# First layer of a two-block network: values stationary for two heads at a time, the gate z computed transposed, and a quarter of the adaLN rows multiplied on TensorE

## The chip, the cores and the metric

The kernel runs on one core of a Trainium2 chip. The metric is the device time of one execution in microseconds (us). The names of the engines are TensorE (PE, matrix products), VectorE (DVE), ScalarE (ACT), GpSimd (POOL) and SyncE (SP, which issues the DMAs here).

## What is computed

Two transformer blocks of two layers each, over 256 tokens of width 1024. The change lies in the mixer of the first layer, and in the rows of modulation that are computed beside it:

```python
def adaln_norm(x, c, g, w_ada, b_ada):
    mod = jax.nn.silu(c) @ w_ada + b_ada
    shift, scale, gate = jnp.split(mod, 3, axis=-1)
    h = rms_norm(x, g) * (1.0 + scale[:, None, :]) + shift[:, None, :]
    return h, gate[:, None, :]

def nsa_mixer(h, w_in, ..., w_out):
    u = h @ w_in
    q, k_c, v_c, k_s, v_s, k_w, v_w, z, g_logit = jnp.split(u, cuts, axis=-1)
...
    o = gates[..., 0:1] * o_cmp + gates[..., 1:2] * o_slc + gates[..., 2:3] * o_win
    o = o.reshape(B, T, ATTN_WIDTH)
    return (o * jax.nn.silu(z)) @ w_out

def first_block(x, c, norm_g, ada_w, ada_b, ...):
    for i in range(DEPTH):
        h, gate = adaln_norm(x, c, norm_g[i], ada_w[i], ada_b[i])
...
        x = x + gate * y
    return rms_norm(x, final_g)
```

The 16 heads of 64 share two groups of keys and values (8 heads each). `o_cmp` is an attention over 15 compressed keys, `o_slc` and `o_win` are here two causal attentions over the 256 tokens with keys and values of their own. All is float32.

## The kernel before

Weights come in units of 512 KB. Each unit is split into a high part (ScalarE, L210) and a low part (VectorE, L211), and the activations are held transposed, split likewise, in one tile `xhl` (channels on partitions). A dense product is three matmuls: high by high, low by high, high by low. `dense_cols` (L239, L240, L243) holds the activations of one token block (128 tokens) stationary and moves 512 columns of weights, so that tokens come out on partitions. `dense_T` (L297 to L299) holds 128 weight columns stationary and moves all 256 tokens, so that the result comes out transposed.

The stage of interest (lines 855 to 935, PSUM banks mm=[0], s=[1,2,3], pt=[4,5], o=[6,7]) computes the first layer's attention for key group g=1, then for g=0. For each group:

- The gate z of 512 columns comes from `dense_cols` (96 matmuls in all for both groups), then silu (ACT, then DVE L550) into `zs`, tokens on partitions.
- `cmp_part` (L885) starts the two accumulators `o` (one bank per token block) with the compressed attention.
- `nsa_pair` runs eight times, for four pairs of heads times two branches. Scores (L450, two heads in the two halves of the rows), mask and maximum (DVE L457), exponential (ACT L463), reciprocal and gate (DVE L894, L896), scaling (128 columns on DVE L904, 256 on ACT L902), then `av` for each head: three transposes (L470), a copy out of PSUM (ACT L473) and three matmuls 128x64 with the probabilities stationary (L476 to L478).
- After each pair, one (g=0) or two (g=1) steps of `ada_rows` make the rows gate0, scale and shift. A step takes a raw tile of 2 x 128 rows of the modulation weights by 512 columns (DMA, L619, three tiles `ar` in a ring) and adds them, scaled by silu(c), to `ac` (DVE L639, L641). Four steps are one half-row. Its end is one matmul by ones (L646), which sums over partitions, and one or two DVE operations (L649, L651, L652).

Then the z of group 1, already multiplied by `o`, and that of group 0 are transposed into `xhl` (`to_T`: L309 on TensorE into a pt bank, L312, L313). The output projection follows (`project_out`, accumulators y=[0,1,2,3], 96 matmuls by L239, L240, L243), the groups' rows 4 to 7 first. Its results go to `nsa_out` (L942 to L955): gate and residual (L378, L379), the norm (ACT L382, L947, POOL L334), scale and shift (L952, L953), transposes (L309), and then the second layer's first dense product.

The order in each engine's queue is set by a tile scheduler, which places instructions by a simulated timeline. `first(...)` gives priority, `behind(...)` puts one instruction after another. Buffers of a pool, PSUM banks among them, are handed out in the order in which the program asks for them. So the projection's products may be placed ahead of attention's last ones wherever their inputs and their banks are free.

## Time and profile before

| what | value |
|---|---|
| median of 3 runs | 999.81 us (993.23 to 1002.75) |
| the profiled execution | 996.02 us |
| its span in the profile | 994.2 us, 1.8 us less than the execution |
| mean granted TensorE clock | 0.978 of full speed |
| instructions | 14760 |
| TensorE busy | 939.6 us |
| VectorE busy | 697.2 us |
| ScalarE busy | 539.7 us |

The stage described above lies between about 96 and 228 us of the span. Times in the rows below are microseconds from the span's start; a line number is that of the listing above. Durations of matmuls overlap each other, since they are pipelined; what one costs is the distance from its start to the next one's. An fp32 matmul leaves two records, which the timeline counts as x2.

### The profile page before, as it was taken

Reading aid. Unit: us, or ns where it says so; the run is one execution under the profiler, and the core shown is the slowest. Engines: PE = TensorE matmul, PEld = TensorE weight load, DVE = VectorE, ACT = ScalarE, POOL = GpSimd, SP = SyncE. Lnnn points to the kernel's source line nnn. Section 1 sums busy time; section 2 is a strip of 40 time slices with the busy share of each in tenths; the row PEclk is TensorE's granted clock in tenths of the full one; section 3 lists DMA queues with packets and bytes.
Section 4 is the critical chain, followed back from the end, with each engine's and each line's share of the span. In section 5 each row is a group of like instructions: output and inputs, shape, how many; then the busy total and the mean of one; then the engine's idle time right before and its main releaser. Section 6 shows DMA issues by size and latency. Waiting matters only on the chain.

```text
span 994.2 us, 14760 instructions
## 1 busy us (share of the span) xinstructions
PE 939.6 (95%) x5316; PEld 787.7 (79%) x5316; DVE 697.2 (70%) x1446; ACT 539.7 (54%) x1062; POOL 40.7 (4%) x49
## 2 busy tenths in 40 slices
PE   5997999999999999999799999999999889999996
PEld 4876786687778877967788888887997688888885
DVE  5878799948786768585857565677466586665655
ACT  5574577834545636586346554435676345555540
POOL 1003000001220001000000000000000000000000
PEclk9998797999999999999999999999999999999999
DMA  9986687334865525732255554644635243564531
GB/s 288 309 290 230 202 278 248 120 107 131 267 198 180 157 59 194 250 114 86 94 203 212 169 184 158 245 177 152 220 130 158 85 169 124 188 239 170 182 136 43
DMA packets 106170, 177.66 MB, mean 179 GB/s; under 512 B 8817, under 2 KB 40689, under 8 KB 106097
## 3 DMA queue, kind: packets, MB, share of 16 engines
q1 hardware_dynamic: 106096, 176.72, 54.2%
q8 instruction: 42, 0.69, 0.3%
q14 instruction: 32, 0.25, 0.1%
HBM read 175.65 MB, written 1.05 MB: 178 GB/s over the span
## 4 chain that ended last, share of the span: by engine, by line
PE 78%; DVE 11%; ACT 4%; DMA 4%; issue 2%; SPq 1%; POOL 0%; DVEq 0%; ACTq 0%; POOLq 0%
PE ps L279 15%; PE ps L239 13%; PE ps L243 13%; PE ps L240 13%; PE ps L280 8%; DMA wr<-in_ada_w_dram 2%; PE ps L450 2%; DVE wl L211 2%; PE ps L320 1%; PE ps L820 1%; PE ps L309 1%; PE ps L506 1%; ACT e L463 1%; PE ps L297 1%; PE ps L298 1%
## 5 line engine op out<-in xcount | busy, mean ns | idle before, releaser
L211 DVE TENSOR_TENSOR wl<-wr,wh 128x1024 fp32r<-128x1024 f32 (+5 forms) x276 | 320.1, 1196 | 78.2 <-ACT wh L210 76.5
L210 ACT ACTIVATE wh<-wr 128x1024 fp32r<-128x1024 f32 (+5 forms) x276 | 270.6, 1021 | 72.9 <-PE ps L243 22.7
L279 PE MATMUL ps<-xhl,wh 128*128 128x512 f32 x640 | 226.5, 398 | 0.0
L239 PE MATMUL ps<-wh,xhl 128*128 128x512 f32 (+5 forms) x544 | 198.8, 379 | 5.1 <-ACT xhl L312 2.5
L240 PE MATMUL ps<-wl,xhl 128*128 128x512 f32 (+5 forms) x544 | 199.7, 370 | 0.0
L280 PE MATMUL ps<-xhl,wl 128*128 128x256 f32 x640 | 179.2, 281 | 0.0
L243 PE MATMUL ps<-wh,xhl 128*128 128x512 f32 (+5 forms) x544 | 173.5, 371 | 0.9 <-DVE xhl L313 0.6
L279 PEld LDWEIGHTS ps<-xhl,wh 128*128 128x128 f32 x640 | 120.0, 188 | 29.0
L239 PEld LDWEIGHTS ps<-wh,xhl 128*128 128x128 f32 x544 | 105.0, 194 | 23.7 <-ACT xhl L312 5.2
L280 PEld LDWEIGHTS ps<-xhl,wl 128*128 128x128 f32 x640 | 120.9, 189 | 1.1
L240 PEld LDWEIGHTS ps<-wl,xhl 128*128 128x128 f32 x544 | 105.2, 193 | 14.5 <-issue 0.5
L243 PEld LDWEIGHTS ps<-wh,xhl 128*128 128x128 f32 x544 | 100.2, 191 | 19.0 <-issue 2.7
L1105 ACT ACTIVATE hs<-ps 128x256 f32<-128x256 f32 x80 | 30.1, 379 | 100.6 <-PE ps L280 100.6
L1106 DVE TENSOR_TENSOR hs<-ps,hs 128x256 f32<-128x256 f32 x80 | 32.7, 421 | 69.4 <-ACT hs L1105 69.4
L243 PE MATMUL ps<-wh,hl 128*128 128x512 f32 x176 | 68.3, 390 | 0.0
L240 PE MATMUL ps<-wl,hh 128*128 128x512 f32 x176 | 68.3, 390 | 0.0
L239 PE MATMUL ps<-wh,hh 128*128 128x512 f32 x176 | 66.6, 390 | 0.0
L463 ACT ACTIVATE e<-e,sm 128x128 f32<-128x128 f32 x112 | 49.6, 445 | 10.4 <-DVE sm L457 10.1
L312 ACT ACTIVATE xhl<-ps 128x512 fp32r<-128x512 f32 x28 | 16.4, 597 | 66.8 <-PE ps L309 66.7
L457 DVE CUSTOM_DVE_ANT_0 e<-ps,mask 128x128 f32<-128x128 f32 (+1 forms) x144 | 44.4, 351 | 9.4 <-PE ps L436 4.6
L641 DVE SCALAR_TENSOR_TENSOR ac<-ar,cs,ac 128x512 f32<-128x512 f32 x56 | 42.7, 764 | 3.9 <-DMA ar<-in_ada_w_dram 3.6
L334 POOL TENSOR_TENSOR sm<-sm,nhalf 128x1 f32<-128x1 f32 x18 | 13.1, 730 | 723.1 <-DVE sm L333 723.1
(314 smaller groups left out, 1297.7 us busy)
## 6 DMA issues: line engine op xcount, KB each, us to landing
wr<-in_ffn_w_gate_dram SPq DMA_DIRECT2D x44, 512.0 KB, 4.5
wr<-in_ffn_w_up_dram SPq DMA_DIRECT2D x44, 512.0 KB, 4.8
wr<-in_ffn_w_down_dram SPq DMA_DIRECT2D x44, 512.0 KB, 4.9
ar<-in_ada_w_dram SPq DMA_DIRECT2D x32, 512.0 KB, 4.5
wr<-in_dil_w_in_dram SPq DMA_DIRECT2D x32, 512.0 KB, 4.7
wr<-in_cd_w_in_dram SPq DMA_DIRECT2D x22, 512.0 KB, 4.3
wr<-in_ada_w_dram SPq DMA_DIRECT2D x32, 256.0 KB, 5.0
wr<-in_nsa_w_in_dram SPq DMA_DIRECT2D x12, 512.0 KB, 5.1
```

The costliest lines, as they stand in the source:

```text
L210: act.activation(hi, raw[:, :nk * n], AF.Copy)
L211: dve.tensor_sub(lo, raw[:, :nk * n], hi.bitcast(F32))
L239: pe.matmul(p, lhsT=xt[0][:, k, :], rhs=w[0][:, kw, c], start=start and t == 0, stop=False)
L240: pe.matmul(p, lhsT=xt[0][:, k, :], rhs=w[1][:, kw, c], start=False, stop=False)
L243: pe.matmul(p, lhsT=xt[1][:, k, :], rhs=w[0][:, kw, c], start=False, stop=stop and t == n - 1)
L279: pe.matmul(p, lhsT=w[0], rhs=xhl[:, k].rearrange("p a t -> p (a t)"), start=k == 0, stop=False)
L280: pe.matmul(p[:, :256], lhsT=w[1], rhs=xh[:, k, :], start=False, stop=k == 7)
L457: state["dve"] = dve.tensor_tensor_reduce(out=e[:, c0:c1], in0=s[:, c0:c1], in1=added[:, 256 - (c1 - c0):], scale=-scale, scalar=3e38, op0 ...
L463: act.activation(e[:, c0:c1], e[:, c0:c1], AF.Exp, bias=n2[:, i:i + 1], scale=-1.0, accum_out=den[:, i:i + 1])
L641: dve.scalar_tensor_tensor(ac, raw[:, j, :], cs[:, k:k + 1], ac, op0=ALU.mult, op1=ALU.add)
L1105: act.activation(t[:, c], p[:, 256:], AF.Copy)
L1106: dve.tensor_add(t[:, c], p[:, :256], t[:, c])
```

## The change

1. z is computed by `dense_T` into `zT` (channels on partitions): 192 matmuls with 256 moving columns in place of 96 with 512. `to_T` on z is gone, `split_T` (L514 on ACT, L515 on DVE) splits `zT` into `xhl` without TensorE or PSUM.
2. `av` becomes `av_pair`, a helper that the later mixers use already. Values are stationary (64 columns), the transposed probabilities of a head move, and the two heads of a pair go to the two halves of the partitions of one bank: 4 matmuls (L506) in place of 6 for a pair, after the same 6 transposes. A bank of `o` now holds two pairs for all tokens, transposed.
3. `cmp_part` has 4 matmuls of 256 moving columns in a group in place of 2 of 512.
4. `ada_rows(..., own=6)`: the last two of the eight row blocks of a half-row are multiplied on TensorE (two fp32 matmuls with silu(c), broadcast over 128 columns, stationary, and the raw tile moving), into the bank where the matmul by ones then adds `ac`. The second layer's later call keeps own=8.

The new numbering moves the lines: L470 is now L495 (the helper's), L904 is L486, L930 is L935, L649 is L653; L646 is the new pair of matmuls and L647 the one by ones.

```diff
--- before.py
+++ after.py
@@ -605,7 +605,7 @@
 
     arow = {}
 
-    def ada_rows(rows, new, ahead):
+    def ada_rows(rows, new, ahead, own=8):
 
 
 
@@ -637,13 +637,17 @@
                     k = u * 2 + j
                     if k == 0:
                         dve.tensor_scalar(ac, raw[:, j, :], cs[:, k:k + 1], None, op0=ALU.mult)
-                    else:
+                    elif k < own:
                         dve.scalar_tensor_tensor(ac, raw[:, j, :], cs[:, k:k + 1], ac, op0=ALU.mult, op1=ALU.add)
+            if u == 3:
+
+                p = ps("pt")
+                for k in range(own, 8):
+                    pe.matmul(p, lhsT=cs[:, k:k + 1].to_broadcast([128, 128]), rhs=raw[:, k % 2, :], start=k == own, stop=False)
+                pe.matmul(p, lhsT=ones, rhs=ac, start=own == 8, stop=True)
             load()
             if u < 3:
                 return
-            p = ps("pt")
-            pe.matmul(p, lhsT=ones, rhs=ac, start=True, stop=True)
             dst, br = arow[name][:, half(h)], at["b"][:, half(h)]
             if at["g"] is None:
                 dve.tensor_add(dst, p, br)
@@ -672,7 +676,7 @@
     vbd = [np_.tile([128, 8, 64], F32, name=f"vbd{g}") for g in range(2)]
     qp = [[np_.tile([128, 4, 128], F32, name=f"qp{t}{g}") for g in range(2)] for t in range(2)]
     qr = [[np_.tile([128, 4, 128], F32, name=f"qr{t}{g}") for g in range(2)] for t in range(2)]
-    zs = [np_.tile([128, D], F32, name=f"zs{t}") for t in range(2)]
+    zT = np_.tile([128, 8, 256], F32, name="zT")
 
 
     cmA, a0 = opened("ada0")
@@ -854,7 +858,7 @@
 
     cmC, pC = opened("nsaC")
 
-    def cmp_probs(tok, g):
+    def cmp_probs(tok, g, t):
         p = ps("s")
         for pr in range(4):
             c = slice(pr * 30, (pr + 1) * 30)
@@ -877,12 +881,19 @@
         dve.tensor_mul(s, s, d8[:, :, None].to_broadcast([128, 8, NCMP]))
         pT = ps("pt")
         pe.transpose(pT[:120, :128], s.rearrange("p h n -> p (h n)"), ident)
-        t = pC.tile([128, 128], F32, tag="cT", bufs=4, name=nm("cT"))
-        act.activation(t[:120], pT[:120, :128], AF.Copy)
-        return t
+        act.activation(t[:120, tok, :], pT[:120, :128], AF.Copy)
+
+    def both_probs(g):
+        t = pC.tile([128, 2, 128], F32, tag="cT", bufs=2, name=nm("cT"))
+        for tok in range(2):
+            cmp_probs(tok, g, t)
+        return t.rearrange("p b t -> p (b t)")
 
     def cmp_part(t, g, o):
-        pe.matmul(o, lhsT=t[:120], rhs=vbd[g][:120].rearrange("p h d -> p (h d)"), start=True, stop=False)
+
+        for pr in range(4):
+            pe.matmul(o[pr // 2][:, (pr % 2) * 256:(pr % 2) * 256 + 256], lhsT=vbd[g][:120, 2 * pr:2 * pr + 2, :].rearrange("p h d -> p (h d)"),
+                      rhs=t[:120], start=pr % 2 == 0, stop=False)
 
     def nsa_pair(g, pr, br, o, last):
 
@@ -896,42 +907,34 @@
         dve.tensor_mul(rd.rearrange("p (j t) -> p j t", j=2), rd.rearrange("p (j t) -> p j t", j=2),
                        gates.rearrange("p t (h b) -> p h b t", b=3)[:, h:h + 2, 1 + br, :])
         for j, e in enumerate(es):
-            for i, (c0, c1) in enumerate(BLOCKS):
-                r = rd[:, 2 * j + i:2 * j + i + 1]
-                if i:
-                    act.activation(e[:, c0:c1], e[:, c0:c1], AF.Copy, scale=r)
-                else:
-                    dve.tensor_scalar(e[:, c0:c1], e[:, c0:c1], r, None, op0=ALU.mult)
-            av(e, lambda b: vv[:, b, g * 64:(g + 1) * 64], o, (pr * 2 + j) * 64, False, act, pC, stop=last and j == 1)
-
-    oxt = [None, None]
+            scaled(e, rd[:, 2 * j:2 * j + 2], (dve, act))
+        av_pair(es, lambda j, b: vv[:, b, g * 64:(g + 1) * 64], o[pr // 2], (pr % 2) * 256, (act, act), pC, False, last)
+
+    oxt = [xt_tiles(0), xt_tiles(1)]
     ada = ada_rows((("gate0", 0, 2 * D), ("scale", 1, D), ("shift", 1, 0)),
-                   lambda: pC.tile([128, D], F32, tag="araw", bufs=ARAW, name=nm("ar")), ARAW)
+                   lambda: pC.tile([128, D], F32, tag="araw", bufs=ARAW, name=nm("ar")), ARAW, 6)
     assign(mm=[0], s=[1, 2, 3], pt=[4, 5], o=[6, 7])
     with first(ATTN):
-        probs = [cmp_probs(tok, 1) for tok in range(2)]
+        probs = both_probs(1)
     for g in (1, 0):
         o = [ps("o"), ps("o")]
-        dense_cols(xt, 8, 512, lambda tok, p: silu2(p, zs[tok][:, half(g)], pC))
+        dense_T(512, lambda pair, p: silu2(p, zT[:, g * 4 + 2 * pair:g * 4 + 2 * pair + 2, :].rearrange("p k t -> p (k t)"), pC))
         with first(ATTN):
-            for tok in range(2):
-                cmp_part(probs[tok], g, o[tok])
+            cmp_part(probs, g, o)
             for i in range(8):
-                nsa_pair(g, i // 2, i % 2, o, i == 7)
+                nsa_pair(g, i // 2, i % 2, o, i in (3, 7))
                 for _ in range(1 + g):
                     ada(state["dve"])
                 if g and i == 3:
-                    probs = [cmp_probs(tok, 0) for tok in range(2)]
+                    probs = both_probs(0)
             if g == 0:
-                oxt = [xt_tiles(0), xt_tiles(1)]
-                for tok in range(2):
-                    to_T(zs[tok][:, half(1)], 4, oxt[tok], 4)
-            for tok in range(2):
-                dve.tensor_mul(zs[tok][:, half(g)], o[tok], zs[tok][:, half(g)])
+                for i in range(2):
+                    split_T(zT[:, 4 + 2 * i:6 + 2 * i, :].rearrange("p k t -> p (k t)"), 4 + 2 * i)
+            for i in range(2):
+                z = zT[:, g * 4 + 2 * i:g * 4 + 2 * i + 2, :].rearrange("p k t -> p (k t)")
+                dve.tensor_mul(z, o[i], z)
                 if g == 0:
-                    to_T(zs[tok][:, half(0)], 4, oxt[tok], 0)
-    for _ in range(24):
-        ada()
+                    split_T(z, 2 * i)
     closed(cmC)
 
     assign(y=[0, 1, 2, 3], pt=[6, 7])
```

How this moves instructions is seen in the engines' queues. In a row stand the line, the operation, output<-inputs with the numbers of the buffers, and the shape (output partitions x columns). `ps` is a PSUM bank, `eT` a head's transposed probabilities, `vS` and `vW` the values of the two branches, `wh` and `wl` the two parts of a weight unit, `cs` silu(c). TensorE in group 0, one pair's scores and a pair's products with the values, before:

```order
L450 MATMUL ps_2026<-kT,qr_114 128x128
L450 MATMUL ps_2025<-kT,qr_114 128x128
L450 MATMUL ps_2026<-kT,qr_116 128x256
L450 MATMUL ps_2025<-kT,qr_116 128x256
L470 MATMUL ps_1951<-ident,e_1936 128x128 x3
L470 MATMUL ps_1962<-ident,e_1942 128x128 x3
L476 MATMUL ps_1791<-vW,eT_1955 128x64
L477 MATMUL ps_1792<-vW,eT_1955 128x64
L478 MATMUL ps_1792<-vW,eT_1955 128x64
```

The same place after:

```order
L450 MATMUL ps_2101<-kT,qr_114 128x128
L450 MATMUL ps_2100<-kT,qr_114 128x128
L450 MATMUL ps_2101<-kT,qr_116 128x256
L450 MATMUL ps_2100<-kT,qr_116 128x256
L506 MATMUL ps_1822<-eT_1992,vS 64x256
L506 MATMUL ps_1822<-eT_1986,vS 64x256
L506 MATMUL ps_1822<-eT_1992,vS 64x128
L506 MATMUL ps_1822<-eT_1986,vS 64x128
L495 MATMUL ps_2038<-ident,e_2021 128x128 x3
```

Six products with the values in a pair (three are shown) have become four, of 64 partitions each, and one bank takes both heads. TensorE at the end of the stage, before:

```order
L646 MATMUL ps_2261<-ac_2118,ones 128x512
L476 MATMUL ps_1791<-vW,eT_2254 128x64
L477 MATMUL ps_1792<-vW,eT_2254 128x64
L478 MATMUL ps_1792<-vW,eT_2254 128x64
L309 MATMUL ps_2264<-ident,zs_118 128x128 x4
L309 MATMUL ps_2271<-ident,zs_119 128x128 x4
L239 MATMUL ps_2300<-wh_1254,xhl 128x512
L240 MATMUL ps_2300<-wl_1255,xhl 128x512
L239 MATMUL ps_2300<-wh_1254,xhl 128x512
```

The end of the stage after:

```order
L646 MATMUL ps_2324<-ar_2192,cs 128x512 x2
L506 MATMUL ps_1823<-eT_2318,vW 64x256
L506 MATMUL ps_1823<-eT_2312,vW 64x256
L506 MATMUL ps_1823<-eT_2318,vW 64x128
L506 MATMUL ps_1823<-eT_2312,vW 64x128
L647 MATMUL ps_2324<-ac_2189,ones 128x512
L239 MATMUL ps_2345<-wh_1921,xhl 128x512
```

Before, all 96 projection matmuls stood behind the last product with the values and behind the transposes of `zs`. After, the transposes are gone, and 72 of the 96 stand ahead of the last pair's products (12 of them ahead of the last pair's scores). TensorE's last rows ahead of the second layer, after:

```order
L243 MATMUL ps_2345<-wh_1921,xhl 128x512 x2
L243 MATMUL ps_2346<-wh_1945,xhl 128x512 x2
L243 MATMUL ps_2347<-wh_1921,xhl 128x512 x2
L243 MATMUL ps_2348<-wh_1945,xhl 128x512 x2
L309 MATMUL ps_2461<-ident,yt_2458 128x128 x4
L309 MATMUL ps_2471<-ident,yt_2468 128x128 x4
L239 MATMUL ps_2577<-wh_2369,xhl 128x512
```

Before, the four accumulators were finished one after the other; now the last eight matmuls finish all of them. VectorE in the last pair, before:

```order
L904 TENSOR_SCALAR e_2184<-e_2184,sm_2170 128x128
L457 ISA e_2230,sm_2229<-ps_2218,mask 128x128
L457 ISA sm_2229 128x1
L457 ISA e_2230,sm_2229<-ps_2218,mask 128x256
L457 ISA sm_2229 128x1
L641 SCALAR_TENSOR_TENSOR ac_2118<-ar_2121,cs,ac_2118 128x512 x2
L894 RECIPROCAL sm_2216<-sm_2215 128x4
L896 TENSOR_TENSOR sm_2216<-sm_2216,gates 128x4
L904 TENSOR_SCALAR e_2224<-e_2224,sm_2216 128x128
L904 TENSOR_SCALAR e_2230<-e_2230,sm_2216 128x128
```

VectorE in the last pair, after:

```order
L457 ISA e_2297,sm_2296<-ps_2285,mask 128x128
L457 ISA sm_2296 128x1
L457 ISA e_2297,sm_2296<-ps_2285,mask 128x256
L457 ISA sm_2296 128x1
L486 TENSOR_SCALAR e_2247<-e_2247,sm_2239 128x128
L486 TENSOR_SCALAR e_2253<-e_2253,sm_2239 128x128
L905 RECIPROCAL sm_2283<-sm_2282 128x4
L907 TENSOR_TENSOR sm_2283<-sm_2283,gates 128x4
L486 TENSOR_SCALAR e_2291<-e_2291,sm_2283 128x128
L486 TENSOR_SCALAR e_2297<-e_2297,sm_2283 128x128
L211 TENSOR_TENSOR wl_2370<-wr_2367,wh_2369 128x1024
```

The two operations L641 of a half-row's fourth step are not there any more; TensorE alone reads that step's raw tile (L646), so it is TensorE that frees it for a later load. VectorE behind the projection, before:

```order
L378 TENSOR_TENSOR yt_2388<-ps_2300,arow_1343 128x512
L379 TENSOR_TENSOR x_69<-x_69,yt_2388 128x512
L378 TENSOR_TENSOR yt_2404<-ps_2301,arow_1343 128x512
L379 TENSOR_TENSOR x_69<-x_69,yt_2404 128x512
```

The same place after:

```order
L378 TENSOR_TENSOR yt_2433<-ps_2345,arow_1389 128x512
L378 TENSOR_TENSOR yt_2449<-ps_2346,arow_1389 128x512
L379 TENSOR_TENSOR x_69<-x_69,yt_2433 128x512
L379 TENSOR_TENSOR x_69<-x_69,yt_2449 128x512
```

Gate and residual of the first token block's two halves now stand side by side, where one half was finished before the other began.

## Rows read from the trace of the kernel before

**Rows 1.** Stretch, its length; busy PE, PEld, DVE, ACT, POOL; granted clock; DMA share, GB/s

```profile
110.40:118.00 7.60, 7.25 (x29) 5.76 (x30) 5.90 (x25) 3.14 (x12) 0.00 (x0) 0.50 0.67 227
118.00:152.80 34.80, 34.80 (x220) 26.57 (x218) 33.77 (x107) 25.70 (x71) 0.00 (x0) 1.00 0.83 271
152.80:156.00 3.20, 1.63 (x12) 1.38 (x11) 3.20 (x7) 2.31 (x7) 0.00 (x0) 0.93 0.80 255
156.00:165.60 9.60, 9.60 (x39) 7.34 (x40) 7.69 (x32) 6.29 (x22) 0.00 (x0) 0.50 0.88 283
165.60:202.90 37.30, 34.01 (x255) 26.08 (x254) 31.34 (x126) 30.24 (x102) 0.00 (x0) 1.00 0.38 119
202.90:228.50 25.60, 25.20 (x122) 20.32 (x121) 15.32 (x23) 8.66 (x14) 0.55 (x1) 1.00 0.34 103
483.20:487.00 3.80, 3.78 (x17) 3.37 (x18) 3.77 (x8) 1.20 (x2) 0.92 (x1) 0.55 0.12 37
```

**Rows 2.** Waits of TensorE from 104 to 230 us, total, times, longest

```profile
PE ps L470 <- DVE zs L550: 1.3, 1, 1.3
```

**Rows 3.** Timeline of TensorE: start, length, instruction; xN records run together

```profile
135.84 0.33 PE L476 MATMUL ps<-vW,eT 128*128 128x64 f32 x2
...
136.45 1.08 PE L646 MATMUL ps<-ac,ones 128*128 128x512 f32 x2
137.36 0.30 PE L861 MATMUL ps<-kbd,qp 128*128 128x30 f32 x2
...
137.78 0.41 PE L476 MATMUL ps<-vW,eT 128*128 128x64 f32 x2
...
138.48 0.50 PE L470 MATMUL ps<-ident,e 128*128 128x128 f32 x3
...
397.68 0.28 PE L297 MATMUL ps<-xhl,wh 128*128 128x256 f32 x1
...
402.95 0.29 PE L299 MATMUL ps<-xhl,wl 128*128 128x256 f32 x1
...
443.34 0.87 PE L506 MATMUL ps<-eT,sv 128*64 128x256 f32 x8
444.14 0.50 PE L243 MATMUL ps<-wh,xhl 128*128 128x512 f32 x1
444.47 0.39 PE L239 MATMUL ps<-wh,xhl 128*128 128x512 f32 x1
```

**Rows 4.** Timeline from the last attention product to the next layer's first product

```profile
202.83 1.04 PE L309 MATMUL ps<-ident,zs 128*128 128x128 f32 x8
204.12 0.50 PE L239 MATMUL ps<-wh,xhl 128*128 128x512 f32 x1 [0.25 <-ACT xhl L312]
...
227.07 1.26 PE L309 MATMUL ps<-ident,yt 128*128 128x128 f32 x8
228.47 0.50 PE L239 MATMUL ps<-wh,xhl 128*128 128x512 f32 x1
...
221.72 0.69 DVE L378 TENSOR_TENSOR yt<-ps,arow 128x512 f32<-128x512 f32 x1 [1.30 <-PE ps L243]
```

**Rows 5.** The same place of the ab mixer, whose attention output is already transposed

```profile
471.23 0.87 PE L506 MATMUL ps<-eT,mv 128*64 128x256 f32 x8
472.80 0.50 PE L239 MATMUL ps<-wh,xhl 128*128 128x512 f32 x1 [0.70 <-ACT xhl L514]
...
478.19 0.39 PE L243 MATMUL ps<-wh,xhl 128*128 128x512 f32 x1
483.22 1.97 PE L309 MATMUL ps<-ident,x 128*128 128x128 f32 x8 [4.64 <-DVE x L367]
485.02 0.58 PE L239 MATMUL ps<-wh,xhl 128*128 128x256 f32 x1
```

**Rows 6.** Vector operations from 152.8 to 202.9 us, by line

```profile
L641 DVE SCALAR_TENSOR_TENSOR ac<-ar,cs,ac 128x512 f32<-128x512 f32 x24 | 17.9, 748 | 0.1
```

**Rows 7.** DMA of the raw adaLN rows from 96 to 204 us

```profile
DMA to landing us min/median/max: 3.6/4.4/6.2
```

## The prediction, made before the changed kernel ran

> **What bounds the kernel now.** TensorE is busy for 939.6 of the 994.2 us of the span, so the first question is where it is not at work, or not at full speed, in the stage that the change touches. I read the stage by stretches [rows 1], then the waits of TensorE [rows 2], then what one instruction costs, as the distance between starts [rows 3]. The reader should see three things. From 118.0 to 152.8 TensorE is busy all the time at granted clock 1.00 (2.4 GHz): there only its own work counts. From 165.6 to 202.9 it is busy for 34.01 of 37.3 us, VectorE for 31.34 and ScalarE for 30.24: a chain through all three engines, in which no single one is full. And in two stretches, 110.4 to 118.0 and 156.0 to 165.6, the granted clock is 0.50 (1.2 GHz). The second follows on an idle time of 1.3 us, in which a transpose L470 waited for the silu of z, VectorE's L550 [rows 2].
>
> I take one stretch for the whole balance, from 110.4 to 228.5, where the second layer's first product starts: 118.1 us. TensorE's idle time in it is length minus busy, row by row: 0.35 + 0 + 1.57 + 0 + 3.29 + 0.40 = 5.6 us. Of 7.6 + 9.6 = 17.2 us at half clock, half is lost: 8.6 us. The remaining 103.9 us are work at full clock. Everything outside the stretch (996.0 - 118.1 = 877.9 us of the profiled execution) I take as unchanged.
>
> **TensorE's work.** All durations are from [rows 3].
> - Products with the values: a head costs 0.61 us (135.84 to 136.45) or 0.70 (137.78 to 138.48), 0.66 as a middle, a pair 1.32. The new form stands in the later mixers: four matmuls L506 (eight records) take 0.80 (443.34 to 444.14). Sixteen pairs save 16 x 0.52 = 8.3 us (6.7 by the short head, 9.6 by the long).
> - Switching the shape of the array: behind such a group the next dense matmul starts 0.33 after the one before it (444.14 to 444.47), where 0.23 is usual (below). That is 0.1 for each pair, +1.6 us; the other end is nothing, since group 0 goes on to other small matmuls.
> - Transposes of z: eight took 1.04 us [rows 4], so the 16 that go save 2.1.
> - z itself: 192 matmuls of 256 columns at 0.120 (44 steps from 397.68 to 402.95) are 23.0; the 96 of 512 that go, at 0.234 (23 steps from 472.80 to 478.19 in [rows 5]), are 22.5. +0.5.
> - The compressed part has half the columns in twice the matmuls; I put it at nothing.
> - adaLN: twelve fp32 matmuls 128x512 more. The trace has none with a broadcast stationary. The matmul by ones has the same size and type, 0.91 (136.45 to 137.36). Bounds are 0.234, the cheap kind of the same size, and 1.82, as if loading the weights took as long again: 2.8 to 21.8 us. I take the nearest row, 0.91: +10.9.
>
> The sum is -8.3 + 1.6 - 2.1 + 0.5 + 10.9 = +2.6 us; TensorE, the fullest engine, gets more work, not less.
>
> Of the switch, the trace shows that the four matmuls and the way into them fit into 0.80 us. The Trainium skill, "TensorEngine Tiling (Array Packing)", Key Properties, says that a change of tiling mode drains TensorE. If each of two changes in a pair exposed a whole matmul latency (0.50 - 0.23 us, by the record at 444.14), that would be 16 x 2 x 0.27 = 8.6 us instead of 1.6, and the forecast 7.0 us later. The 0.33 us agrees with some drain, of a smaller size.
>
> **VectorE's work.** Twelve L641 of 0.748 us go [rows 6]: -9.0 us. Before 152.8 TensorE is full, so nothing comes of it there. Behind it, ScalarE's 30.24 us and TensorE's own work are next in line, so I leave the idle time of that chain at 3.29 us; the other end is that it vanishes. The raw tile of the fourth step is now freed by TensorE. A raw tile lands 3.6 to 6.2 us after its issue [rows 7]; three tiles are in the ring, so a step has about two others to cover that. In the queue the two matmuls stand in the middle of their pair, next to the preceding pair's products, and need no sum of VectorE's, so I price this at nothing; the cover is thin, and the second rival is what it costs without it.
>
> **The end of the stage.** Before, the path from the last product with the values ran 202.83 to 228.47, 25.6 us: transposes, 96 projection matmuls, transposes, next layer [rows 4]. After, 72 of the 96 stand ahead of that product, since their input needs no PSUM bank any more and the first half of it is ready when the second half's attention still runs. The ab mixer already has this form [rows 5]: last L506 at 471.23, a wait of 0.70 for the split, 24 matmuls to 478.4, an idle time of 4.64 for the norm, transposes. Here the norm differs. From the gate of token block 0's second half, L378 at 221.72, to the transposes at 227.07 it took 5.35 us [rows 4]. After, the gate and residual of both halves stand in front of it, 2 x 0.69 = 1.4 more, but the first starts some six matmuls (1.4 us) before the last one. I take 5.0, between 4.64 and 5.35. So the end is 0.70 + 5.6 + 5.0 + 1.4 (transposes to product, 227.07 to 228.47) = 12.7 us. Half of 25.6, but the 72 matmuls (16.8 us) are work still, only elsewhere; what is new in the balance is idle time of 0.70 + 5.0 = 5.7 in place of 0.40. The shorter end hides no VectorE work that was free before.
>
> **The sum.** Work 103.9 + 2.6 = 106.5. Idle 0.35 + 3.29 + 5.7 = 9.3, the 1.57 before the second slow spell being gone, since z's products of group 0 are spread over the pairs of group 1. Lost at half clock: the first spell's 3.8 stays; the second's 4.8 goes with the wait. Together 119.6, against 118.1: +1.5 us. On the profiled execution's own 996.0 this is 997.5 us. The median of the three runs is 999.8, 3.8 us above that execution; I do not add it. For this kernel a measurement can tell about 1% from no change, 10 us.
>
> **Rivals.**
> 1. Faster, the gaps fill. z's small matmuls also stand in the gaps ahead of 110.4, so the first slow spell may not come (-3.8); VectorE's 9.0 us empty the chain's gaps (-3.29); the work comes at its low end without switches (-2.9: long head and no switch). 997.5 - 10.0 = 987.5. For it: VectorE's L641 was the largest single group in that chain, 17.9 us [rows 6]. Against it: from 118 to 165.6 the DMA engines have a share of 0.80 to 0.88 [rows 1], so raw tiles come little sooner, and the three would all have to happen.
> 2. Slower, TensorE holds the raw tiles. If the two matmuls run more than a step behind VectorE, the ring's next load starts late; it lands 4.4 us later, two steps of two L641 each cover 3.0, and 1.4 us are left in which VectorE stands, with the reciprocal and the scaling of a pair queued behind L641, and TensorE behind these. That is the size of wait (1.3) after which the clock was at half for 9.6 us, 4.8 lost. So 6.2 us each time, and in group 1, with two steps a pair, there are three half-rows that another follows: two such events give 997.5 + 12.4 = 1009.9, one gives 1003.7. [...]
> 3. The clock falls at the new idle end. After the 4.64 us of ab the next product ran at granted clock 0.55 for 3.8 us (the last row of [rows 1]), 1.7 lost; 4.8 if it lasts like the spell at 156. 999.2 to 1002.3. The Trainium skill, "TensorE: Matmul & The Clock Gate", Part 1, has the throttled clock as the default that activity releases; that agrees with the row.
> 4. The change is a mere displacement: work comes out even, and idle time moves from the middle to the end. 996.0.
> 5. Each way into and out of the four matmuls exposes a whole latency, 0.27 us, 32 times: 8.6 us in place of 1.6, 1004.5. Against it: the 0.80 and 0.33 us of [rows 3].
>
> **Chances.** Forecast 0.33, rival 1 0.22, rival 2 0.15, rival 3 0.15, rival 4 0.10, rival 5 0.05. The forecast's own range is 988 (rival 1's terms) to 1004 (the wait of rows 2 comes back: 1.3 + 4.8). The broadcast matmul's bounds shift it by 8.1 down and 10.9 up. The range is 984 to 1010. Faster by over 1% needs rival 1 and a little more, or runs that lie as low as the profiled one: 0.22. Slower by over 1% is rival 2 with two events, or the dear matmul: 0.16. Within 1%: 0.62.
>
> **What would show it.** Right: L506 groups of 0.8 us, the broadcast matmuls at 0.9, VectorE 9 us less busy, an end of about 13 us from the last L506 to the next layer with some 5 us idle before L309, no half clock after 150. Wrong: TensorE waiting for L486 or L905 next to late raw tiles (rival 2); no half clock at all and a stage that reaches the second layer before 222 us (rival 1); broadcast matmuls far from 0.9.

## The result, and the profile after

The changed kernel took 1005.17 us (median of 22 runs, 1001.62 to 1007.72), the kernel before 998.03 in the same comparison (993.23 to 1003.90). The ratio is 1.0069, with an interval of 1.0053 to 1.0085: slower by 0.7%, where the forecast had 997.5 us. The profiled execution took 1007.39 us, its span is 1005.6.

The page of the changed kernel, busy us by engine and the granted clock in 40 slices of the span:

```profile
PE 943.7 (94%) x5364; PEld 786.2 (78%) x5364; DVE 690.3 (69%) x1434; ACT 539.2 (54%) x1062; POOL 40.6 (4%) x49
...
PEclk9998799998999999999899999999999979999999
```

VectorE's busy time fell from 697.2 to 690.3 us, TensorE's rose from 939.6 to 943.7. The same stretches as in [rows 1], in the columns stretch, length, busy PE, PEld, DVE, ACT, POOL, granted clock, DMA share, GB/s:

```profile
110.40:118.00 7.60, 7.17 (x38) 6.33 (x38) 5.75 (x25) 2.80 (x11) 0.00 (x0) 0.50 0.70 240
118.00:152.80 34.80, 33.13 (x241) 24.86 (x241) 30.49 (x105) 23.57 (x73) 0.00 (x0) 0.99 0.81 257
152.80:168.40 15.60, 13.86 (x101) 10.29 (x99) 12.58 (x33) 11.10 (x29) 0.00 (x0) 1.00 0.54 182
168.40:180.00 11.60, 11.04 (x57) 6.27 (x58) 9.13 (x38) 8.17 (x27) 0.00 (x0) 0.85 0.76 249
180.00:218.10 38.10, 37.03 (x221) 25.30 (x221) 24.20 (x88) 27.27 (x81) 0.00 (x0) 1.00 0.39 126
218.10:226.20 8.10, 7.67 (x35) 5.21 (x34) 3.33 (x6) 0.63 (x1) 0.00 (x0) 1.00 0.25 72
226.20:233.20 7.00, 1.87 (x9) 1.61 (x9) 4.82 (x10) 1.93 (x5) 0.55 (x1) 0.65 0.00 0
233.20:236.00 2.80, 2.80 (x10) 2.25 (x10) 2.80 (x5) 1.32 (x3) 0.00 (x0) 0.66 0.00 0
```

The stage now ends at 233.2 (228.5 before). From 110.4 on, TensorE's idle time by row is 0.43 + 1.67 + 1.74 + 0.56 + 1.07 + 0.43 + 5.13 = 11.0 us, 5.6 before. Low clock stands in the first row, as before, in part of the fourth and in the last two. The waits of TensorE from 90 to 240 us (total, times, longest):

```profile
PE ps L309 <- issue: 5.2, 1, 5.2
PE ps L495 <- DVE arow L655: 1.7, 1, 1.7
...
PE ps L297 <- DVE zT L550: 0.8, 1, 0.8
```

The wait of 1.3 us for L550 in [rows 2], which was to go, has shrunk to 0.8, but one of 1.7 us for the row of scale (L655) has come, and the clock was low just behind it, at 170 to 174. The trace shows why it came:

```profile
163.50 1.02 PE L647 MATMUL ps<-ac,ones 128*128 128x512 f32 x2
...
167.67 0.68 DVE L655 SCALAR_TENSOR_TENSOR arow<-ps,ab 128x512 f32<-128x512 f32 x1
168.41 0.55 PE L495 MATMUL ps<-ident,e 128*128 128x128 f32 x3 [1.75 <-DVE arow L655]
```

The sum was ready by 164.5, but VectorE went without a pause through two weight splits (L211), one `split_T` (L515) and one L641 before it read the sum (L655), and L655 is what the trace names as the releaser of the transposes L495. The prices of the new instructions, against [rows 3]:

```profile
130.37 0.87 PE L506 MATMUL ps<-eT,vS 128*64 128x256 f32 x8
131.17 0.55 PE L495 MATMUL ps<-ident,e 128*128 128x128 f32 x3
...
133.94 1.88 PE L646 MATMUL ps<-ar,cs 128*128 128x512 f32 x4
135.65 1.02 PE L647 MATMUL ps<-ac,ones 128*128 128x512 f32 x2
136.60 0.65 PE L506 MATMUL ps<-eT,vW 128*64 128x256 f32 x4
```

The products of a pair take 0.80 us (130.37 to 131.17), two broadcast matmuls 1.71 (133.94 to 135.65), so 0.86 each, and the matmul by ones 0.95. VectorE's share, against [rows 6]:

```profile
L641 DVE SCALAR_TENSOR_TENSOR ac<-ar,cs,ac 128x512 f32<-128x512 f32 x30 | 22.4, 747 | 2.7 <-DMA ar<-in_ada_w_dram 2.5
```

30 in the whole stretch, 42 before: twelve are gone. The end of the stage, against [rows 4] and [rows 5]:

```profile
218.11 0.87 PE L506 MATMUL ps<-eT,vW 128*64 128x256 f32 x8
...
220.43 0.50 PE L239 MATMUL ps<-wh,xhl 128*128 128x512 f32 x1 [0.40 <-ACT xhl L514]
...
224.20 1.98 PE L243 MATMUL ps<-wh,xhl 128*128 128x512 f32 x8
231.33 1.94 PE L309 MATMUL ps<-ident,yt 128*128 128x128 f32 x8 [5.16 <-issue]
233.16 0.79 PE L239 MATMUL ps<-wh,xhl 128*128 128x512 f32 x1
...
224.85 1.29 DVE L378 TENSOR_TENSOR yt<-ps,arow 128x512 f32<-128x512 f32 x2 [3.49 <-PE ps L243]
226.06 1.28 DVE L379 TENSOR_TENSOR x<-x,yt 128x512 f32<-128x512 f32 x2
228.14 0.16 DVE L950 TENSOR_TENSOR sm<-sm 128x1 f32<-128x1 f32 x1 [0.80 <-ACT junk L382]
...
229.21 1.41 DVE L955 SCALAR_TENSOR_TENSOR yt<-x,sm,arow 128x512 f32<-128x512 f32 x2 [0.73 <-POOL sm L334]
```

From the end of the last L506 (218.11 + 0.80) to the second layer (233.16) are 14.3 us, 12.7 were forecast; a matmul by ones stands in between. The idle time ahead of the transposes is 5.16 us, 5.0 were forecast. The rows of VectorE show what fills it: gate and residual of both halves, and the norm. The first products behind it run at half clock: L309 takes 1.94 us where [rows 4] has 1.26.

### The profile page after: what moved, and what is told of

It reads as the page before. It is cut to its first block, busy times and chain, and to the rows that moved or that the text cites. A ratio compares the mean times of both kernels' runs of the same rounds, so it can differ in the third digit from the quotient of the medians.

```text
span 1005.6 us, 14837 instructions
## 1 busy us (share of the span) xinstructions
PE 943.7 (94%) x5364; PEld 786.2 (78%) x5364; DVE 690.3 (69%) x1434; ACT 539.2 (54%) x1062; POOL 40.6 (4%) x49
## 4 chain that ended last, share of the span: by engine, by line
PE 78%; DVE 10%; DMA 4%; ACT 4%; issue 3%; SPq 1%; POOL 0%; DVEq 0%; ACTq 0%; POOLq 0%
PE ps L279 15%; PE ps L239 13%; PE ps L240 13%; PE ps L243 13%; PE ps L280 8%; PE ps L450 2%; PE ps L506 2%; DMA wr<-in_ada_w_dram 2%; PE ps L297 2%; PE ps L495 2%; DVE wl L211 2%; PE ps L299 2%; PE ps L298 2%; PE ps L320 1%; ACT wh L210 1%
## 5 line engine op out<-in xcount | busy, mean ns | idle before, releaser
L211 DVE TENSOR_TENSOR wl<-wr,wh 128x1024 fp32r<-128x1024 f32 (+5 forms) x276 | 320.2, 1196 | 80.1 <-ACT wh L210 78.0
L239 PE MATMUL ps<-wh,xhl 128*128 128x512 f32 (+5 forms) x512 | 186.4, 377 | 5.5 <-ACT xhl L312 2.5
L240 PE MATMUL ps<-wl,xhl 128*128 128x512 f32 (+5 forms) x512 | 189.7, 373 | 0.0
L280 PE MATMUL ps<-xhl,wl 128*128 128x256 f32 x640 | 179.2, 281 | 0.0
L243 PE MATMUL ps<-wh,xhl 128*128 128x512 f32 (+5 forms) x512 | 164.5, 373 | 0.8 <-DVE xhl L313 0.6
L239 PEld LDWEIGHTS ps<-wh,xhl 128*128 128x128 f32 x512 | 98.9, 195 | 23.2 <-ACT xhl L312 4.5
L240 PEld LDWEIGHTS ps<-wl,xhl 128*128 128x128 f32 x512 | 101.1, 197 | 13.3 <-issue 0.3
L243 PEld LDWEIGHTS ps<-wh,xhl 128*128 128x128 f32 x512 | 96.7, 196 | 16.5 <-DVE xhl L313 1.9
L312 ACT ACTIVATE xhl<-ps 128x512 fp32r<-128x512 f32 x24 | 14.2, 597 | 66.5 <-PE ps L309 55.0
L297 PE MATMUL ps<-xhl,wh 128*128 128x256 f32 x160 | 48.0, 300 | 0.8 <-DVE zT L550 0.8
L299 PE MATMUL ps<-xhl,wl 128*128 128x256 f32 x160 | 47.1, 294 | 0.9 <-DVE wl L211 0.9
```

What stands on the lines that cost most here:

```text
L211: dve.tensor_sub(lo, raw[:, :nk * n], hi.bitcast(F32))
L239: pe.matmul(p, lhsT=xt[0][:, k, :], rhs=w[0][:, kw, c], start=start and t == 0, stop=False)
L240: pe.matmul(p, lhsT=xt[0][:, k, :], rhs=w[1][:, kw, c], start=False, stop=False)
L243: pe.matmul(p, lhsT=xt[1][:, k, :], rhs=w[0][:, kw, c], start=False, stop=stop and t == n - 1)
L280: pe.matmul(p[:, :256], lhsT=w[1], rhs=xh[:, k, :], start=False, stop=k == 7)
L297: pe.matmul(o, lhsT=w[0], rhs=xh[:, k, :], start=k == 0, stop=False)
```

## Experiments

Two theories stood at first. A: the loss is TensorE's work for the adaLN rows. C: it is the new end. The expectations name rivals by letters too: B, VectorE is as full as TensorE there; D, the idle time only moves; E, what costs is that TensorE holds the raw tile and a bank. Besides the ratio of each run there is a narrower measure, the length of the stage in its one profiled execution: from the first product of the scores (L450, at 111.09 in the changed kernel, 110.75 before) to the second layer's first product. "Block 0 first" is the edit of run 4 below.

| run | median us | ratio, interval | stage us |
|---|---|---|---|
| before | 998 | | 117.7 |
| changed (own=6) | 1005.17 | 1.0069, 1.0053 to 1.0085 | 122.1 |
| 1: own=8 | 1000.84 | 1.0023, 1.0001 to 1.0046 | 117.1 |
| 2: before, own=6 alone | 1004.48 | 1.0065, 1.0038 to 1.0092 | 120.7 |
| 3: projection behind | 1002.52 | 1.0039, 1.0018 to 1.0059 | 119.3 |
| 3a: both 1 and 3 | 1000.28 | 1.0020, 0.9997 to 1.0042 | 116.4 |
| 4: block 0 first | 1000.72 | 1.0016, 0.9987 to 1.0045 | 118.0 |
| 4a: both 1 and 4 | 998.22 | 0.9989, 0.9953 to 1.0026 | 113.7 |
| 4a again | 997.78 | 0.9999, 0.9978 to 1.0021 | 114.4 |
| 5: own=7 | 1002.68 | 1.0026, 0.9996 to 1.0055 | 118.8 |
| 6: thin broadcast, behind | 1003.74 | 1.0032, 1.0001 to 1.0064 | 121.4 |
| 6a: thin broadcast, in place | 999.71 | 0.9990, 0.9968 to 1.0011 | 116.9 |
| 6b: own=8 and a thin read | 1004.12 | 1.0052, 1.0025 to 1.0079 | 120.9 |
| 7: bank of the scores | 1002.85 | 1.0041, 1.0021 to 1.0060 | 125.2 |
| 8: own=6 beside group 0, block 0 first | 999.35 | 1.0012, 0.9993 to 1.0031 | 116.5 |
| 8a: own=6 beside group 1, block 0 first | 999.51 | 1.0021, 1.0002 to 1.0040 | 115.9 |
| 8b: own=6 beside group 0, projection behind | 1002.68 | 1.0046, 1.0025 to 1.0067 | 119.6 |
| 9: GpSimd, block 0 first | 1006.73 | 1.0081, 1.0050 to 1.0112 | 123.3 |

Medians of different rows come from different hours; the ratios compare each with the kernel before on its own chip. A stage holds what its one execution lost to a low clock; the two of 4a differ by 0.7 us, and for run 7 stage and ratio point opposite ways.

**Runs 1 and 2: the adaLN rows alone.** Run 1 edits the changed kernel as below; run 2 gives the kernel before the new `ada_rows` with own=6, and nothing else:

```diff
-                   lambda: pC.tile([128, D], F32, tag="araw", ...), ARAW, 6)
+                   lambda: pC.tile([128, D], F32, tag="araw", ...), ARAW, 8)
```

> The changed kernel with own=8: the twelve broadcast matmuls go back to twelve L641 on VectorE, all else as changed. Theory A (the loss is TensorE's extra work for the adaLN rows, 12 x 0.9 = 10.9 us on the fullest engine): about 6 to 9 us less than the changed kernel, 996 to 999 us, VectorE 9 us more busy. Rival B (VectorE is as full as TensorE there, the 9.0 us come back on its side): 1004 to 1006, no difference from the changed kernel. Theory C (the loss is the new end, 5.2 us of idle time and the half clock behind it) says nothing of this part alone: the gap of about 5 us before the transposes stays in either case.

> The kernel before with own=6 alone: values, z and the end as before. Theory A: 4 to 9 us slower than before, 1002 to 1007 us. Rival B: VectorE's relief pays for TensorE's work, within 2 us of before, or faster. Theory C: no difference from before, since the end is the old one.

Taking the twelve matmuls out of the changed kernel gives back 4.6 thousandths (1.0069 to 1.0023) and 5.0 us of the stage; putting them into the kernel before costs 6.5. Theory A's size is right for run 2 and too large for run 1 (4.3 us between the medians, expected were 6 to 9), B falls. But own=8 is still no faster than before, though against the kernel before 8.9 us of TensorE's work are away (the balance below). Idle time took their place: 6.2 us more at the new end and some 4 in the chain ahead of it, as in the stretch from 155 to 170 of run 1 (columns as above):

```profile
155.00:170.00 15.00, 11.23 (x80) 7.38 (x78) 14.95 (x42) 12.22 (x34) 0.00 (x0) 1.00 0.90 295
```

VectorE is busy for 14.95 of 15 us, TensorE for 11.23.

**Runs 3 and 4: the end.** Run 3 puts every projection matmul behind the last product with the values. Run 4 leaves the early ones and puts only token block 1's last twelve behind those of block 0:

```diff
-                products(accs[tok][h], ..., start=not last, stop=last == 1, ...)
+                products(accs[tok][h], ..., start=not last, stop=last == 1, ...,
+                         late=state["mm0"] if late and last and tok else None)
+                if not tok:
+                    state["mm0"] = state["mm"]
```

where `late` stands ahead (`behind`) of the last two of four terms, and `state["mm"]` is the last matmul made.

> The changed kernel with all 96 projection matmuls behind the last product with the values, so that token block 0's accumulators are finished ahead of block 1's, as before. Theory C: the gap of 5.2 us before the transposes and the half clock behind it go, the last product with the values comes near 203 us instead of 218, and the second layer starts near 228 to 229 instead of 233: 997 to 1001 us. Rival D (the gap only moves: TensorE waits in the attention for what the early projection filled): last product with the values near 207 or later, 1003 to 1007 us.

> Both at once: own=8 and the projection behind the last product with the values. Theories A and C together: 988 to 994 us, faster than both kernels. B and D: no better than the better one of the two single edits, 997 or more.

> The changed kernel, with token block 1's last 12 projection matmuls behind block 0's last one, so that block 0's two accumulators are finished 12 matmuls (2.7 us) ahead of the end. The early projection stays. Theory C (the end's idle time is a loss of its own): the gap of 5.2 us before the transposes falls to some 2.5 to 3 and the half clock behind it shortens or goes; 1000.5 to 1003 us against 1005.2 for the changed kernel. Rival D (the gap only moves): 1004 to 1006.

> The same order of the last 24 matmuls with own=8. Theories A and C add up: 1000.8 (own=8 alone) less 2.5 to 4.5, 996 to 998.5 us, at or a little below the kernel before. Rival D: 1000 to 1001.5.

Run 3 lies between C and D, and with own=8 it adds almost nothing (1.0023 to 1.0020). The last product with the values came at 204.7, near C's 203, but what the early projection had filled was then idle, as D has it (8.8 us up to there, 5.5 in the changed kernel up to 218.1). Run 4 is C's clean form, and within its bounds: the idle time ahead of the transposes falls from 5.16 to 3.35 us,

```profile
225.72 1.67 PE L311 MATMUL ps<-ident,yt 128*128 128x128 f32 x8 [3.35 <-issue]
227.10 0.79 PE L240 MATMUL ps<-wh,xhl 128*128 128x512 f32 x1
```

and the stage by 4.1 us with own=6 and 3.4 with own=8 (table). By the ratios the order in which the last 24 matmuls finish the accumulators costs 5.3 thousandths with own=6 and 2.4 to 3.4 with own=8.

Runs 1 and 4 add up by the stage: with both, 113.7 us, 4.0 less than before; the end's order adds 3.4 (117.1), the adaLN rows 5.0 more (122.1). That is the whole change: -4.0 + 3.4 + 5.0 = +4.4 us. But 3.3 of the 4.0 us are low clock, of which before's profiled execution had more (8.7 us lost, 5.4 in run 4a's). By idle time and work alone (the balance below) the three steps are -0.9, +2.2 and +5.4: +6.7 us, of which the adaLN rows are the largest part.

**Run 5: half the rows.** `ARAW, 7)` in place of 6.

> The changed kernel with own=7: one row block of eight on TensorE, six broadcast matmuls in place of twelve. Theory A (each costs its time on TensorE, and VectorE's relief pays only part of it): half way between own=6 (1005.2) and own=8 (1000.8), 1002 to 1004 us. Rival B (two engines out of balance, an optimum between): below both, 999 or less.

It lies between own=8 and own=6, in stage and ratio, as A expected; no optimum between shows.

**Run 6: TensorE's time, or the hold?** The broadcast matmuls are cut to 64 of 512 columns, so that most of their products are left out: first behind the matmul by ones (run 6), then ahead of it as in the changed kernel (run 6a, the edit below, cut; a cheap bf16 matmul fills the bank first), then with own=8 (run 6b):

```diff
-                for k in range(own, 8):
-                    pe.matmul(p, lhsT=cs[:, k:k + 1].to_broadcast([128, 128]), rhs=raw[:, k % 2, :], ...)
-                pe.matmul(p, lhsT=ones, rhs=ac, start=own == 8, stop=True)
...
+                pe.matmul(p, lhsT=identb, rhs=identb[:, None, :].to_broadcast([128, 4, 128]), start=True, stop=False)
+                for k in range(6, 8):
+                    pe.matmul(p[:, 0:64], lhsT=cs[:, k:k + 1].to_broadcast([128, 128]), rhs=raw[:, k % 2, 0:64], ...)
+                pe.matmul(p, lhsT=ones, rhs=ac, start=False, stop=True)
...
```

> The changed kernel, in which the twelve broadcast matmuls read and add only the first 64 of 512 columns (behind the matmul by ones), so most of rows 6 and 7 of each eight is left out of gate0, scale and shift. TensorE's price is nearly gone, VectorE's relief of 9.0 us stays. Theory A: TensorE's 12 x 0.9 us were what cost, so 7 to 10 us below the changed kernel, 995 to 998. By its distance to own=8 (1000.8) VectorE's relief is measured: if it is worth nothing, 1000 to 1001.5; if VectorE is as full as TensorE (B), 992 to 995.

> As the run that cut the broadcast matmuls to 64 of 512 columns, but with these in the changed kernel's place ahead of the matmul by ones (behind a cheap bf16 matmul that fills the bank), so that the raw tile and the bank are held as in the changed kernel and only TensorE's time goes (6 x some 1.3 us, 8 us). Most of rows 6 and 7 of each eight is left out of gate0, scale and shift. Theory A (TensorE's time is what costs): 996 to 999 us. Theory E (not the time, but that TensorE holds the raw tile and one of two pt banks): 1002 to 1005, no more than 3 below the changed kernel.

> own=8, so VectorE does all rows again, and in addition TensorE reads 64 columns of each fourth step's raw tile ahead of the matmul by ones, as above: TensorE's cheap time (some 0.5 us, six times) and the hold, without VectorE's relief. Identity and some columns are added to gate0, scale and shift, which the result shows. Theory A: 1001 to 1003.5, at most 3 above own=8 alone (1000.8). Theory E: 1004 to 1008, since the raw tile and the bank are now held by both engines.

Run 6 surprised: TensorE's price was nearly gone, and yet only 3.7 thousandths came back, with the stage hardly shorter. For a moment theory A seemed to fall. Its trace shows more waiting for raw tiles (idle time of an engine before instructions on them, us and times; run 6, then run 6a):

```profile
  DMA ar<-in_ada_w_dram: 5.8, 3
...
  DMA ar<-in_ada_w_dram: 4.2, 2
```

(2.5 us in two waits in the changed kernel.) Behind the sum, TensorE can free the raw tile only when VectorE's whole half-row is done. But run 6a waits nearly as long and is faster, so this is not the whole of it: by the balance of its execution run 6 has 2.0 us more idle time on TensorE than run 6a and loses 3.3 us more to low clock. What of that comes of the place is not shown. Run 6a keeps the place and cuts the time; the group takes 0.71 us (131.21 to 131.92), 1.0 less than the two full matmuls:

```profile
131.21 0.39 PE L646 MATMUL ps<-identb 128*128 128x512 bf16 x1
131.44 0.55 PE L648 MATMUL ps<-ar,cs 128*128 128x64 f32 x4
131.92 0.87 PE L506 MATMUL ps<-eT,vW 128*64 128x256 f32 x8
132.72 1.13 PE L649 MATMUL ps<-ac,ones 128*128 128x512 f32 x2
```

It is 7.9 thousandths below the changed kernel, for six times 1.0 us removed. So theory A holds, and by the ratio TensorE's time counts in full; by the balance (below) 7.2 us of work went, 3.1 came back as idle time, and 3.1 less was lost to low clock. Run 6b adds six times 0.71 = 4.3 us to own=8 and costs 2.9 thousandths, as A expected at most, though its median, 1004.12, reaches E's range. Between 6b and 6a VectorE's twelve operations go and nothing else: 6.2 thousandths, some 6 of their 9.0 us. In the two profiled executions TensorE's idle time and work are the same within 1 us, and the difference is low clock alone (8.0 us lost in 6b, 3.6 in 6a), so how much of the 6 us is VectorE's relief is not settled.

**Run 7: the bank.** The half-row's sum takes a bank of the scores:

```diff
-                p = ps("pt")
+                p = ps("s" if own < 8 else "pt")
```

> The changed kernel, with the sum of a half-row in one of the three banks of the scores instead of one of the two of the transposes; nothing else. Theory E, by the bank: the waits of the transposes L495 and of the broadcast matmuls for a pt bank go, 1000 to 1003 us. Theory A, or E by the raw tile alone: 1004 to 1006.5, or more, where the scores now wait for a bank.

By the ratio 2.8 thousandths better than the changed kernel (the intervals overlap), by its one profiled execution a longer stage. Inconclusive; it can't be told whether the bank plays a part.

**Run 8: by place.** `own = least if name == "shift" else 8` (group 0), or `!=` (group 1).

> own=6 for the rows of shift alone (the two half-rows that are made beside group 0, four broadcast matmuls), own=8 for gate0 and scale (beside group 1), and block 0's accumulators finished first. Theory A by place (a broadcast matmul costs its time where TensorE is full, beside group 1, and little beside group 0, where TensorE waits for ScalarE and VectorE): 995 to 998 us, as good as own=8 in that order (998.2, ratio 0.9989) or up to 3 us better. Theory A without place (each costs the same): a third of the difference of own=6 and own=8 in that order, 998.5 to 999.5.

> The other way round: own=6 for gate0 and scale, beside group 1 (eight broadcast matmuls), own=8 for shift. Theory A by place: the whole loss of own=6 in that order is here, 1000 to 1002 us (own=6 throughout 1000.7, ratio 1.0016). Without place: two thirds of it, 999 to 1000.

> own=6 for the rows of shift alone, with the whole projection behind the last product with the values, so that TensorE has idle time beside group 0. Theory A by place: VectorE's relief counts there and TensorE's time does not, 996 to 999 us, below own=8 in that form (1000.3, ratio 1.0020). Without place: 1000.5 to 1001.5.

Nothing speaks for "by place". Both partial forms lie between own=8 and own=6 in the stage (113.7, 116.5, 115.9, 118.0), the four matmuls beside group 0 as dear there as the eight beside group 1; and where TensorE had idle time (8b against 3a) they cost 2.6 thousandths all the same. The differences of the ratios lie within their intervals, so this is weaker than runs 1 and 2. That an engine with idle time in a stretch isn't free there can be argued: a half-row's 1.7 us of matmuls stand ahead of transposes and scores for which VectorE waits.

**Run 9: GpSimd.** Block 0 first, own=8, but

```diff
+                    elif k >= 6 and ahead == ARAW and name != "gate1":
+                        pool.tensor_tensor(raw[:, j, :], raw[:, j, :], cs[:, k:k + 1].to_broadcast([128, 512]), op=ALU.mult)
+                        pool.tensor_tensor(ac, ac, raw[:, j, :], op=ALU.add)
```

> own=8 with block 0's accumulators finished first, but the last two row blocks of each half-row (rows 6 and 7 of 8, gate0, scale and shift) multiplied and added on GpSimd, two operations each of some 1.8 us (the size of its additions in the profile of before), 24 in all, 43 us on an engine that is idle there. TensorE gets no work and VectorE loses 9.0 us. If VectorE's relief is worth the 3 to 6 us that the cheap broadcast showed: 992 to 996 us, faster than both kernels. If the half-rows now come too late, or VectorE is slowed by GpSimd: 998 or more.

> The kernel with own=8 and block 0's accumulators finished first once more, with more rounds, beside the former: 996 to 999 us, ratio 0.998 to 1.000 if the first measurement (0.9989, 0.9953 to 1.0026) holds.

The slowest of all, against an unchanged reference. The groups of GpSimd and VectorE in this run (line engine operation, shapes, count, busy us, mean ns):

```profile
L647 POOL TENSOR_TENSOR ac<-ac,ar 128x512 f32<-128x512 f32 x12 | 17.4, 1453 | 9.4 <-PE ps L500 4.2 <-DVE sm L913 2.9 <-DVE sm L915 1.2
L646 POOL TENSOR_TENSOR ar<-ar,cs 128x512 f32<-128x512 f32 x12 | 15.6, 1323 | 68.3 <-DMA ar<-in_ada_w_dram 26.6 <-PE ps L300 26.0 <-DVE sm L878 9.4
...
L491 DVE TENSOR_SCALAR e<-e,sm 128x128 f32<-128x128 f32 x32 | 14.4, 490 | 0.2
```

Its stretch from 140 to 170:

```profile
140.00:170.00 30.00, 25.82 (x199) 19.56 (x196) 29.33 (x81) 19.32 (x55) 10.30 (x8) 0.94 0.70 224
```

And VectorE's scaling in the same kernel without GpSimd (run 4a):

```profile
L491 DVE TENSOR_SCALAR e<-e,sm 128x128 f32<-128x128 f32 x32 | 7.7, 286 | 0.1
```

VectorE lost twelve operations and is busy for 29.3 of 30 us; several of the others got longer (the last section). Of the 10.1 us by which the balance of this execution is longer than run 4a's, 6.9 are low clock (12.3 us lost, 5.4 in run 4a's) and 3.9 idle time of TensorE.

## Why the prediction was wrong

Forecast were +1.5 us; it came to +4.7 by the end of the stage (233.16 against 228.47) and +7.1 by the medians. The measured time lies in the range, and within 1% was the likeliest class, but the loss is clear of its interval and the forecast was next to no change.

The prediction's balance, from 110.4 to the second layer's first product, can be drawn up for each profiled execution: idle is length less busy time of TensorE; lost is TensorE's busy time times what the granted clock lacked of 1.00, summed by microsecond; work is the rest.

| us | length | idle | lost to low clock | work |
|---|---|---|---|---|
| before | 118.1 | 5.6 | 8.7 | 103.7 |
| forecast | 119.6 | 9.3 | 3.8 | 106.5 |
| changed | 122.8 | 11.0 | 6.7 | 105.0 |
| 1: own=8 | 117.6 | 15.8 | 7.0 | 94.8 |
| 2: before, own=6 alone | 120.2 | 4.6 | 2.9 | 112.7 |
| 4a: own=8, block 0 first | 113.8 | 13.4 | 5.4 | 95.0 |
| 6: thin broadcast, behind | 120.3 | 16.1 | 6.9 | 97.2 |
| 6a: thin broadcast, in place | 115.4 | 14.1 | 3.6 | 97.8 |
| 6b: own=8 and a thin read | 120.2 | 13.8 | 8.0 | 98.5 |
| 9: GpSimd, block 0 first | 123.9 | 17.3 | 12.3 | 94.3 |

**The step that failed: "Lost at half clock: the first spell's 3.8 stays; the second's 4.8 goes with the wait."** 6.7 us were lost, 2.9 more than forecast, the largest part of the 3.2 us by which the stage missed. The wait for L550 shrank, but a wait of 1.7 us for the row of scale took its place, and 1.7 us were lost behind it (168.4 to 180.0, granted clock 0.85). Run 2 agrees that the spell goes where the wait goes: there the wait for L550 is 0.2 us, and 2.9 us are lost in the whole stretch. What failed is that no other wait of that size would come. Without this credit of 4.8 us the forecast's own terms, +2.6 of work and +3.7 of idle time, give +6.3 us. The other part is rival 3: the first products behind the new idle end ran at half clock, 0.9 us to 233.2 and 1.0 behind it (the last row, 0.66).

**Work** was right: 105.0, forecast 106.5. Its terms hold one by one, too. Without the adaLN rows it is 94.8, 8.9 less than before, for which the prediction had 8.3; with them 10.2 more, for which it had 10.9 (a matmul takes 0.86, not 0.91).

**Idle time: 11.0, forecast 9.3, and wrong in its reasons.** "I leave the idle time of that chain at 3.29 us" hides two errors of opposite sign. Of the 15.8 us of run 1, the end has 1.5 and 5.1, so 9 are left for the chain, 5.2 before: nearly half of what TensorE saved at the values and z became waiting. 152.8 to 168.4 of run 4a shows on what, VectorE busy for 14.93 of 15.6 (the second row is run 4a's end):

```profile
152.80:168.40 15.60, 11.80 (x83) 8.10 (x83) 14.93 (x43) 12.81 (x34) 0.00 (x0) 1.00 0.89 296
...
211.70:224.20 12.50, 7.70 (x40) 5.76 (x36) 7.48 (x13) 2.56 (x6) 0.55 (x1) 0.97 0.19 72
```

"From 118.0 to 152.8 ... only its own work counts" was right for the kernel before, and no longer when TensorE had less to do (it is idle for 1.8 us there in runs 1 and 4a): VectorE's 33.77 of 34.80 stood in the same row [rows 1]. Then idle time falls again, 15.8 to 11.0 us, from run 1 to the changed kernel, where TensorE gets its twelve matmuls and VectorE loses twelve operations. So 10.2 us of work cost 5.2 us of length, and 4.6 thousandths by the ratios. Which of the two takes the idle time away isn't shown; runs 6b and 6a, with VectorE's operations and without, have the same (13.8 and 14.1), which speaks for TensorE's own work.

**The end** came as forecast in kind and size (idle time 5.16, forecast 5.0), and as a cost. Run 4 shows what of it was avoidable: 3.4 to 4.1 us of the stage.

**Rival 1** (faster) didn't come: the first slow spell stayed (granted clock 0.50 from 110.4 to 118.0). **Rival 2** (TensorE holds the raw tiles) was real in kind: waits for raw tiles rose from 0.8 to 2.5 us, and to 5.8 in run 6, where the matmuls stand later. They are not what decides: run 6a waits 4.2 us for them and is faster than the changed kernel. **Rival 5** (dear switches) didn't come: 0.80 us for a group, as in the later mixers. The Trainium skill, "TensorEngine Tiling (Array Packing)", Key Properties, has a drain at each change of mode; no run here measures it alone.

**The rest of the 7.1 us, and what stays open.** The two profiled spans differ by 11.4 us: 7.2 are idle time, 1.2 work and 3.0 low clock. From the second layer's first product to the end, length less what low clock cost is 762.6 us before and 762.9 changed; the low clock there cost 3.2 and 9.6 us. Nothing ties the difference to the change: over all profiled executions the low clock there costs between 3.2 and 12.1 us. Before's is the least; it is 9.3 in run 2, which has the old end, and 4.4 in run 7, which has the new one. Executions at the same mean granted clock, 0.975 to 0.977, say what is left: the median is 999.2 us in 26 of the kernel before, from all later comparisons, and 1005.1 in 13 of the changed one. These 5.9 us are near the 6.7 of idle time and work in the stage. Run 4a has a stage 3 to 4 us shorter than before and the same time, at median clocks of 0.974 and 0.975 against 0.976 and 0.978; at the same clock its ten executions lie some 2 us below before's. Why its clock is lower isn't shown, nor what VectorE's relief alone is worth. No version beat the kernel before beyond its interval.

## What to carry to other kernels

Work taken from the fullest engine counts only up to the next engine's busy share in the same stretch: read the row's other columns before booking it, for here VectorE had 33.8 of 34.8 us beside a full TensorE. When work moves between two engines that alternate in one chain, price both ends (here 10.2 us more on one and 9.0 less on the other came to 5 us more) and not just the one that looks full. And do not book a low-clock spell of one execution as saved because its wait goes, before asking which wait comes next. Where early fill lets several accumulators finish together, look at which one the next step needs, and finish that one first.

## Not expected of the hardware

**GpSimd slows VectorE.** In run 9 GpSimd's additions took 1.45 us and its products 1.32. VectorE lost twelve operations, yet its scaling L491 (128x128) took 490 ns, against 286 in run 4a without GpSimd. Within run 9 it shows that GpSimd is the cause: the 11 of these that overlap one of the 24 GpSimd operations took 893 ns in the mean, the 21 others 280. The weight splits L211 took 1604 (4) and 1220 (8). The masking L462, which reads PSUM, did not change (342 and 350). What GpSimd took over, VectorE lost again in its other operations: its busy time in the execution is 703.7 us, 696.6 in run 4a. The Trainium skill, "SBUF — State Buffer", Who interferes with whom, has the two engines share a pair of ports that one holds alone; the run agrees with that.

**The same idle time, a different spell.** Behind the 4.64 us of idle time of the ab mixer [rows 5] the clock was low for 3.4 us in the profiled execution of before (1.7 us lost), for 7.0 in the changed kernel's (3.0) and for 10.2 in run 4a's (3.9, as the spell began while TensorE was still idle), though the instructions there are the same. By such differences one kernel's executions spread (993 to 1004 us), and a change of a few us is read from idle time and work, or from executions at the same granted clock, and not from single times.
